# A hybrid decoder layer in float32 on one core: two-operand work moved from GpSimd to VectorE, scan outputs issued later, and four PSUM banks for the gated state-space projection

## The chip, the cores and the metric

The kernel runs on one core of a Trainium2 chip. A core has five engines, each with its own queue of instructions that it works off in order: TensorE (PE, matmuls into PSUM banks), VectorE (DVE), ScalarE (ACT), GpSimd (POOL) and SyncE (SP, which issues transfers). They meet only through semaphores, so an instruction that waits holds up all that stands behind it on its engine. The metric is the time on the device in microseconds, the median of several runs.

## What is computed

A layer with a residual stream of 1024 positions by 1024 channels, all in float32:

```python
mod = silu(c) @ W_ada + b_ada          # shift, scale, gate for two sub-layers
u = rmsnorm(h) * g_mix * (1 + scale1) + shift1
q, k, v, u_ssm, g_att, g_ssm = split(u @ w_in)
y_att = dilated_window_attention(q, k, v) @ w_proj_att     # three patterns, 8 heads
y_ssm = s5(u_ssm) @ w_proj_ssm         # complex diagonal scan, gelu, GLU
merged = sigmoid(g_att) * y_att + sigmoid(g_ssm) * y_ssm
h = h + gate1 * (merged @ w_out)
u = rmsnorm(h) * g_ffn * (1 + scale2) + shift2
a, val = split(u @ w_up)               # 2 x 2048
h = h + gate2 * ((silu(causal_conv3(a)) * val) @ w_down)
out = rmsnorm(h) * g_final
```

## The kernel before

**Float32 products.** [...] So each operand is split into a high part, which ACT makes by a copy with rounding, and a low part, the difference, made by a subtraction with two operands. A product is then three matmuls into one bank (`mm3`, L185): high by high, high by low, low by high (L187 to L189). Every weight goes through this: class `Weights` loads item after item (`_load_to`), splits it two items ahead of its use (`_parts`: ACT at L123, the low part at L124), and chooses the engine for the low part at L111: VectorE for some of the out projection's items, GpSimd for all others.

**Order.** Nothing is scheduled by a tool; the order on each engine is the order in which the program issues. A `Builder` keeps a clock in estimated microseconds (`unit`, L152). The main line of the program adds to it with every group of matmuls, and generators in the background (`spawn`, with a delay) put in their instructions when the clock passes their next due time.

**Stages**, by the time in the trace:

- 0 to 75 us, first products: a loop over 8 channel chunks k (L380). `prep_a(k)` makes the scale of the chunk: `row_dot`, a dot product of a row of `W_ada` with silu(c) on DVE (`ada_dot`, L1413), the bias added (L328), the column `gs` (L346); then ACT scales x by it into the high part of `xg` (L318) and squares x (L355), and GpSimd adds the squares up (L357). `split_w` makes the weights' parts, the low one on GpSimd (L309). `prep_b(k)` makes the low part of `xg` on DVE (L361). PE then does seven groups, 21 matmuls, for the chunk. Eight more dots for the shift come in late (`DOTS`; one of them, `POOL_DOTS`, is multiplied on GpSimd). A matmul with ones (L368) adds up the squares over the partitions, `newton` makes the root, and the bias products (L443) follow.
- 75 to 131: the normalised input u, and its value, query and key products. 134 to 356: attention.
- 356 to 485: gates and projections of the attention branch, in the order g0 g1 g2 p0 p1 p2 g3 p3 and so on to g7 p7. A projection takes its bank (`ps_s`, two of them) and DVE multiplies it into `Tm` (L639). In the background runs the S5 branch: its scan is small DVE instructions (L1736 to L1740) for two halves of the channel groups, one after the other; `outputs(q)` turns the scan's states into outputs on PE (L1749, L1750, the latter reads the scan's result L), and then follow transfers and the gelu.
- 485 to 610: gates of the state-space branch, the GLU, and the merge: `proj_ssm` (L699) takes a bank, multiplies it by the gate (L709), adds `Tm` (L710), and splits the result into high (L711, ACT) and low (L713 on GpSimd, L717 on DVE for the last two tiles). Dots for the second modulation (`adaB`) run on DVE in the background.
- 610 to 700: out projection in two halves; `residual` (L835) adds it to the stream and sums squares (`acc`, L847, on GpSimd there). 700 to 748: first feed-forward blocks and `norm2` for the second half, with low parts (`op_lo`, L825) partly on GpSimd.
- 748 to the end: the feed-forward part by Strassen's scheme, bound by PE, and the final norm.

PSUM has eight banks, two for each of the tags mm, s, t and o (L174).

Of the kernel before, what the change touches and what calls it, by code (L numbers as in the profile page):

```python
# [39 lines left out]
LAG2 = 2  # L40
LOP = (4, 5, 6, 7)
U2A, U2B = 7.5, 3.0
ADA1 = 8.0
FIN, LATE_ACC = 5.0, 3
PREP = 4
# [26 lines left out]
class Weights:  # L72
# [139 lines left out]
def body(tc, I, O, dbg=None):  # L212
    b = Builder(tc, I, O)
    nc = tc.nc
    with ExitStack() as ctx:
# [88 lines left out]
        def split_w(i):  # L304
            raw = raws.pop(i)
            w = b.whl.tile([P, 2, 1024], R32, name="whl", tag="whl") if i in (0, 1, 5) else b.A([P, 2, 1024], R32, "whA")
            for cs in halves if i == 0 else [slice(0, 1024)]:
                nc.scalar.activation(w[:, 0, cs], raw[:, cs], AF.Copy)
                nc.gpsimd.tensor_sub(w[:, 1, cs], raw[:, cs], w[:, 0, cs].bitcast(F32))  # L309
# [10 lines left out]
        def row_dot(j):  # L320
            row = rows.pop(j)
            if j in POOL_DOTS:
                nc.gpsimd.tensor_mul(row, row, csil)
                nc.scalar.activation(row, row, AF.Copy, accum_out=mod[:, j:j + 1])
            else:
                ada_dot(nc, mod, j, row, csil)
            if j >= KT:
                nc.vector.tensor_add(mod[:, j:j + 1], mod[:, j:j + 1], cols[:, j:j + 1])  # L328

# [12 lines left out]
        w0, xg = [], {}  # L342

        def prep_a(k):
            row_dot(KT + k)
            nc.vector.tensor_scalar(gs1[:, k:k + 1], mod[:, KT + k:KT + k + 1], 1.0, cols[:, C_GMIX + k:C_GMIX + k + 1],  # L346
                                    op0=OP.add, op1=OP.mult)
            if k == 0:
                xg_hi(0, halves[:1])
            if k % 2 == 0:  # L350
                w0.append(split_w(k // 2))
            if k:
                xg_hi(k, [slice(0, S)])
            sq = sqp[:, 1 if k else 0]
            nc.scalar.activation(sq, xs[k], AF.Square)  # L355
            if k > 0:
                nc.gpsimd.tensor_add(sqp[:, 0], sqp[:, 0], sq)  # L357

# [13 lines left out]
        late = {}  # L372
        for fn, at in ((row_dot, DOTS), (stats, STATS)):
            for a, kn in enumerate(at):
                late.setdefault(kn, []).insert(0, (fn, a))
# [4 lines left out]
        for k in range(KT):  # L380
# [55 lines left out]
        load_w(6)  # L436
        list(newton[0])

# [261 lines left out]
        def proj_ssm(m, wp, c0):  # L700
# [3 lines left out]
            for hf in range(2):  # L704
                hs = slice(hf * HF, (hf + 1) * HF)
                ps = b.ps("s")
                b.run(b.group(ps, wp, 2, Z, hf, c0))
# [128 lines left out]
        def residual(src, x, m, gate, hs, first, last):  # L836
# [7 lines left out]
            if last:  # L844
                ends.setdefault(hs.start, []).append(sq)
            else:
                (nc.vector if gate == 40 and m % ND >= LATE_ACC else nc.gpsimd).tensor_add(acc[:, hs], sq, acc[:, hs])  # L847

        def norm2(n, hf, tiles, low):

# [8 lines left out]
            if n >= LAG2:  # L859
                op_lo(*tiles[n - LAG2], nc.gpsimd if n - LAG2 in low else nc.vector)  # L860

        def gen_u2a():
# [7 lines left out]
            for n in range(KT + LAG2):  # L870
                norm2(n, 0, tiles, ())
                yield 3.0

        def gen_u2b():
# [17 lines left out]
            for k in range(4):  # L892
# [727 lines left out]
class S5:  # L1620
# [5 lines left out]
    def chain(self, coeff):  # L1626
# [275 lines left out]
```

## Time and profile before

| | |
|---|---|
| Three runs | 1199.57, 1201.26, 1202.49 us; median 1201.26 |
| The profiled execution | 1198.02 us; its span in the trace 1196.2 us |
| Mean clock granted to PE | 0.978 |
| DMA | 155.00 MB, mean 130 GB/s |
| POOL in slices 1 to 10 (tenths busy, 40 slices of 29.9 us) | 5553245545 |

A row of the timeline gives the start, the duration, the engine, the line of the kernel, the operation, the tiles (out<-in) and shapes; in brackets stands how long the engine had been idle before it and what ended that (`<-` engine, tile, line). A row of the list of waits gives the total, the number and the longest. A row of the windows gives the stretch, its length, the busy time of PE, of weight loads (PEld), DVE, ACT and POOL with the number of instructions, then the granted clock, the DMA share and GB/s.

### The profile page before, as it was taken

To read this page: it belongs to the slowest core of one execution; us is meant where nothing else is said; L and a number is where in the kernel's file an instruction comes from. 1 tells how busy PE (TensorE), PEld (TensorE's weight loads), DVE (VectorE), ACT (ScalarE), POOL (GpSimd) and SP (SyncE) were. 2 spreads that over 40 slices of the span, in tenths; PEclk is the share of its full clock that TensorE was granted. 3 is DMA by queue.
4 is the path that set the end of the run, shared out by engine and by line. 5 is a ranking of instruction groups with operands and counts; after the bars stand their busy time and mean duration, and the time that the engine had idled before them with its cause. 6 is when DMAs were issued, how large, how long until landed. Compare 5 with 4: busy or idle time off the path is not lost.

```text
span 1196.2 us, 14783 instructions
## 1 busy us (share of the span) xinstructions
PE 1123.7 (94%) x5276; PEld 920.5 (77%) x5276; DVE 890.0 (74%) x1606; ACT 573.9 (48%) x1041; POOL 323.4 (27%) x259
## 2 busy tenths in 40 slices
PE   8779999999999977999999999899999999999995
PEld 6547788888878866877778887688888888887784
DVE  6898677877549597246876758978886777979767
ACT  4334677777852312332233554644543446635653
POOL 5553245545422211224633653000000000000115
PEclk9889999999999988999999999899999999999998
DMA  9410211111123212125458360254533327769433
GB/s 376 172 36 18 80 53 36 52 38 54 36 63 86 49 58 72 47 102 162 143 185 309 102 229 36 73 174 148 186 125 123 103 84 258 277 230 375 168 124 140
DMA packets 56184, 155.00 MB, mean 130 GB/s; under 512 B 7312, under 2 KB 13584, under 8 KB 54320
## 3 DMA queue, kind: packets, MB, share of 16 engines
q1 hardware_dynamic: 46368, 140.37, 33.1%
q10 hardware_dynamic: 9744, 13.70, 3.6%
q8 instruction: 41, 0.67, 0.2%
q14 instruction: 31, 0.25, 0.1%
HBM read 122.00 MB, written 31.46 MB: 128 GB/s over the span
## 4 chain that ended last, share of the span: by engine, by line
PE 60%; DVE 23%; ACT 8%; issue 3%; DMA 3%; POOL 1%; SPq 0%; DVEq 0%; ACTq 0%; POOLq 0%
PE ps_s L1259 13%; PE ps_mm L1259 9%; PE ps_t L1259 8%; PE ps_mm L187 6%; PE ps_mm L189 6%; PE ps_mm L188 6%; DVE ada L1413 3%; PE ps_s L187 2%; PE ps_s L188 2%; PE ps_s L189 2%; DVE tt L1738 2%; DMA xk<-in_xT 1%; DVE op L825 1%; PE ps_t L1552 1%; ACT S L1528 1%
## 5 line engine op out<-in xcount | busy, mean ns | idle before, releaser
L1259 PE MATMUL ps_s<-op,half 128*128 128x512 f32 x792 | 189.5, 390 | 2.9 <-ACT ps_s L1273 1.9
L1259 PEld LDWEIGHTS ps_s<-op,half 128*128 128x128 f32 x792 | 148.4, 188 | 35.3 <-ACT ps_s L1273 3.2
L124 POOL TENSOR_TENSOR whl<-wraw,whl 128x256 fp32r<-128x256 f32 (+2 forms) x68 | 102.3, 1505 | 197.8 <-ACT whl L123 191.3
L847 POOL TENSOR_TENSOR acc<-tp,acc 128x512 f32<-128x512 f32 x22 | 31.7, 1443 | 455.6 <-ACT tp L843 455.5
L187 PE MATMUL ps_mm<-u,whl 128*128 128x512 f32 x360 | 144.5, 401 | 0.0
L189 PE MATMUL ps_mm<-u,whl 128*128 128x512 f32 x360 | 141.1, 392 | 0.0
L188 PE MATMUL ps_mm<-u,whl 128*128 128x512 f32 x360 | 141.0, 392 | 0.0
L1259 PE MATMUL ps_mm<-op,half 128*128 128x512 f32 x528 | 127.9, 395 | 2.9 <-DVE f L964 2.9
L1259 PEld LDWEIGHTS ps_mm<-op,half 128*128 128x128 f32 x528 | 100.6, 191 | 24.5 <-ACT half L1064 3.3
L1259 PE MATMUL ps_t<-op,half 128*128 128x512 f32 x432 | 103.9, 389 | 0.7 <-ACT tp L1267 0.7
L1259 PEld LDWEIGHTS ps_t<-op,half 128*128 128x128 f32 x432 | 81.0, 188 | 17.9 <-ACT tp L1267 1.1
L189 PEld LDWEIGHTS ps_mm<-u,whl 128*128 128x128 f32 x360 | 67.9, 188 | 14.9
L187 PEld LDWEIGHTS ps_mm<-u,whl 128*128 128x128 f32 x360 | 68.1, 189 | 12.0 <-issue 1.0
L188 PEld LDWEIGHTS ps_mm<-u,whl 128*128 128x128 f32 x360 | 68.1, 189 | 10.5
L1557 DVE TENSOR_TENSOR PT<-ps_t,PT 128x512 fp32r<-128x512 f32 (+1 forms) x80 | 50.6, 633 | 28.5 <-ACT PT L1555 27.8
L1065 DVE TENSOR_TENSOR half<-scr,half 128x512 fp32r<-128x512 f32 x80 | 54.5, 684 | 16.3 <-ACT half L1064 16.1
L1532 POOL TENSOR_SCALAR S<-S,mcol 128x128 f32<-128x128 f32 (+3 forms) x64 | 48.8, 765 | 50.7 <-DVE mcol L1531 28.7
L123 ACT ACTIVATE whl<-wraw 128x256 fp32r<-128x256 f32 (+2 forms) x73 | 49.7, 681 | 23.0 <-PE ps_s L189 19.0
L1528 ACT ACTIVATE S<-S,mcol 128x128 f32<-128x128 f32 (+3 forms) x64 | 49.3, 771 | 14.7 <-DVE mcol L1526 13.1
L1413 DVE CUSTOM_DVE_ANT_0 ada<-ada,cpage 128x1024 f32<-128x1024 f32 x23 | 51.0, 2238 | 5.5 <-DMA ada<-in_wada 5.5
L1064 ACT ACTIVATE half<-scr 128x512 fp32r<-128x512 f32 x80 | 49.0, 625 | 8.6 <-DVE scr L1046 5.5
L1065 DVE TENSOR_TENSOR half<-wraw,half 128x512 fp32r<-128x512 f32 x66 | 45.0, 685 | 8.8 <-ACT half L1064 8.8
(490 smaller groups left out, 2555.3 us busy)
## 6 DMA issues: line engine op xcount, KB each, us to landing
wraw<-in_wup SPq DMA_DIRECT2D x32, 512.0 KB, 3.6
fq<-f SPq DMA_DIRECT2D x16, 1024.0 KB, 5.6
ft<-fq SPq DMA_DIRECT2D x14, 1024.0 KB, 7.5
ada<-in_wada SPq DMA_DIRECT2D x24, 512.0 KB, 8.5
wraw<-in_wdn SPq DMA_DIRECT2D x20, 512.0 KB, 5.7
adaB<-in_wada ACTq DMA_DIRECT2D x16, 512.0 KB, 4.0
wraw<-in_wout SPq DMA_DIRECT2D x16, 512.0 KB, 3.6
hd<-h SPq DMA_DIRECT2D x12, 512.0 KB, 7.5
```

The lines of the kernel that those rows point to most:

```text
L123: nc.scalar.activation(w[:, 0, cs], raw[:, cs], AF.Copy)
L124: lo.tensor_sub(w[:, 1, cs], raw[:, cs], w[:, 0, cs].bitcast(F32))
L187: nc.tensor.matmul(ps, wh, xh, start=first, stop=False)
L188: nc.tensor.matmul(ps, wh, xl, start=False, stop=False)
L189: nc.tensor.matmul(ps, wl, xh, start=False, stop=last)
L1064: nc.scalar.activation(w[:, 0], src, AF.Copy)
L1065: lows.append(lambda: nc.vector.tensor_sub(w[:, 1], src, w[:, 0].bitcast(F32)))
L1259: mm = lambda wp, xp, i: nc.tensor.matmul(ps, w[:, wp, ws], xp[:, cs], start=first and k + i == 0, stop=k == KT // 2 - 1 and i == 2, skip_ ...
L1413: nc.vector.tensor_tensor_reduce(out=a, in0=a, in1=csil, op0=OP.mult, op1=OP.add, scale=1.0, scalar=0.0, accum_out=mod[:, j:j + 1])
L1528: nc.scalar.activation(tl, tl, AF.Exp, bias=mc[:, 0:1], scale=-1.0, accum_out=mc[:, 2:3])
L1532: nc.gpsimd.tensor_scalar(tl, tl, mc[:, 3:4], 0.0, op0=OP.mult, op1=OP.add)
L1557: 0, lambda: nc.vector.tensor_sub(pt[:, 1, :w], tps[:, :w], pt[:, 0, :w].bitcast(F32)))
```

## The change

Six parts; line numbers are those of the kernel before unless they stand in a fence of the order after.

a. **First products.** The low parts of weights (L309) are made on DVE. For the chunk pairs after the first, `split_hi` issues ACT's half ahead of the dot and hands the DVE half back to be issued after `gs`. The square additions (L357) go to DVE, one chunk later (`lag1`). The bias and the one of the scale are added once for all chunks (`base`), so L328 goes. The dot on GpSimd goes to DVE. The first `newton` is issued within the last chunk.

b. **Weights.** From item `i_mrg + 4` on (the gates g3 to g7 of the state-space branch, its projections, the out projection and the first four up items) the low part L124 is made on DVE.

c. **Merge.** `proj_ssm` takes its two halves' banks from two tags, s and t, so four banks in turn; all low parts of `merged` go to DVE, each issued after the next half's multiplication and addition.

d. **Residual.** All square additions L847 go to DVE.

e. **Norm 2.** The low parts that were on GpSimd (four of the second half, four of T2) go to DVE, those of T2 one step later.

f. **Scan outputs.** `outputs(0)` is spawned 12 units after its scan instead of 2, `outputs(1)` 24 after its own, where it was run in line after 2.

```diff
-S5_LAG, S5_Y = 2.0, 2.0
+S5_LAG, S5_Y = 2.0, (12.0, 24.0)
...
-            lo = nc.vector if self.small + 1 < self.ns < self.small + KT + 1 else nc.gpsimd
+            lo = nc.vector if self.ns >= self.vec else nc.gpsimd
...
+        W.wide, W.small, W.vec = i_up, i_out, i_mrg + 4
...
-                nc.gpsimd.tensor_sub(w[:, 1, cs], raw[:, cs], w[:, 0, cs].bitcast(F32))
+                nc.vector.tensor_sub(w[:, 1, cs], raw[:, cs], w[:, 0, cs].bitcast(F32))
...
+        def split_hi(i):
+            raw = raws.pop(i)
+            w = b.whl.tile([P, 2, 1024], R32, name="whl", tag="whl") if i == 1 else b.A([P, 2, 1024], R32, "whA")
+            nc.scalar.activation(w[:, 0], raw, AF.Copy)
+            return w, lambda: nc.vector.tensor_sub(w[:, 1], raw, w[:, 0].bitcast(F32))
...
+        base = pg1.tile([P, KT], F32, name="base")
+        nc.vector.tensor_scalar(base, cols[:, KT:2 * KT], 1.0, None, op0=OP.add)
+        def square(k):
+            sq = sqp[:, 1 if k else 0]
+            nc.scalar.activation(sq, xs[k], AF.Square)
+            if k:
+                lag1.append(lambda: nc.vector.tensor_add(sqp[:, 0], sqp[:, 0], sq))
...
         def prep_a(k):
+            low = None
+            if k and k % 2 == 0:
+                w, low = split_hi(k // 2)
+                w0.append(w)
             row_dot(KT + k)
...
-            if k > 0:
-                nc.gpsimd.tensor_add(sqp[:, 0], sqp[:, 0], sq)
+            if low:
+                low()
+            for fn in lag1:
+                fn()
+            lag1.clear()
+            square(k)
...
-                ps = b.ps("s")
+                ps = b.ps("t" if hf else "s")
...
-                if m < 6:
-                    nc.gpsimd.tensor_sub(mt[:, 1, hs], t, mt[:, 0, hs].bitcast(F32))
-                else:
-                    for fn in lows:
-                        fn()
-                    lows[:] = [lambda mt=mt, t=t, hs=hs: nc.vector.tensor_sub(mt[:, 1, hs], t, mt[:, 0, hs].bitcast(F32))]
+                for fn in lows:
+                    fn()
+                lows[:] = [lambda mt=mt, t=t, hs=hs: nc.vector.tensor_sub(mt[:, 1, hs], t, mt[:, 0, hs].bitcast(F32))]
...
-                (nc.vector if gate == 40 and m % ND >= LATE_ACC else nc.gpsimd).tensor_add(acc[:, hs], sq, acc[:, hs])
+                nc.vector.tensor_add(acc[:, hs], sq, acc[:, hs])
...
-                op_lo(*tiles[n - LAG2], nc.gpsimd if n - LAG2 in low else nc.vector)
+                op_lo(*tiles[n - LAG2], nc.vector)
...
-            if q == 0:
-                b.spawn(outputs(0), S5_Y)
-        yield S5_Y
-        yield from outputs(1)
+            b.spawn(outputs(q), S5_Y[q])
```

How the order on the engines moves is shown at three places. First VectorE in the first products, one chunk of the loop before and two after; before, a chunk is the dot (an ISA instruction and the read of its sum), the bias, `gs` and the low part of `xg`:

```order
L1413 ISA ada,mod<-ada,cpage 128x1024
L1413 ISA mod 128x1
L328 TENSOR_TENSOR mod<-mod,cols 128x1
L346 TENSOR_SCALAR gs_115<-mod,cols 128x1
L361 SCALAR_TENSOR_TENSOR xg<-xk,gs_115,xg 128x1024
```

and after, two chunks, one with a weight to split and one without:

```order
L1427 ISA ada,mod<-ada,cpage 128x1024
L1427 ISA mod 128x1
L360 TENSOR_SCALAR gs_115<-mod,base,cols 128x1
L317 TENSOR_TENSOR whA<-wvx,whA 128x1024
L352 TENSOR_TENSOR sq<-sq 128x1024
L376 SCALAR_TENSOR_TENSOR xg<-xk,gs_115,xg 128x1024
L1427 ISA ada,mod<-ada,cpage 128x1024
L1427 ISA mod 128x1
L360 TENSOR_SCALAR gs_115<-mod,base,cols 128x1
L352 TENSOR_TENSOR sq<-sq 128x1024
L376 SCALAR_TENSOR_TENSOR xg<-xk,gs_115,xg 128x1024
```

The bias row is gone; ahead of each low part of `xg` now stands the square addition (`sq`), and in every second chunk the low part of a weight (`whA`) as well.

Second TensorE at the outputs of the second scan (`ps_t<-L,Vt` reads the scan's result); before, the second group of four stands within the sixth attention projection (`ps_s<-Oat`), and the gate products of g7 (`ps_mm<-u`) follow it:

```order
L187 MATMUL ps_s<-Oat,whl 128x512
L188 MATMUL ps_s<-Oat,whl 128x512
L189 MATMUL ps_s<-Oat,whl 128x512
L1749 MATMUL ps_t<-U_3619,TP 128x128
L1750 MATMUL ps_t<-L,Vt 128x127
L1749 MATMUL ps_t<-U_3619,TP 128x128
L1750 MATMUL ps_t<-L,Vt 128x127
```

after, the outputs stand behind the gate products of the first state-space gate:

```order
L186 MATMUL ps_mm<-u,whl 128x512
L187 MATMUL ps_mm<-u,whl 128x512
L188 MATMUL ps_mm<-u,whl 128x512
L1763 MATMUL ps_t<-U_3612,TP 128x128
L1764 MATMUL ps_t<-L,Vt 128x127
L1763 MATMUL ps_t<-U_3612,TP 128x128
L1764 MATMUL ps_t<-L,Vt 128x127
```

Between the two places lie the rest of the sixth projection, g7, the whole seventh projection and half of that gate, all of which PE now does ahead of the outputs.

Third VectorE in the merge, from one pair of banks to the next; before, a half is a multiplication out of the bank and the addition of `Tm`, with dots (`adaB`) between:

```order
L709 TENSOR_TENSOR sg<-ps_s,sg 128x512
L710 TENSOR_TENSOR sg<-sg,Tm 128x512
L1413 ISA adaB,mod<-adaB,cs 128x1024
L1413 ISA mod 128x1
L709 TENSOR_TENSOR sg<-ps_s,sg 128x512
L710 TENSOR_TENSOR sg<-sg,Tm 128x512
```

after:

```order
L724 TENSOR_TENSOR sg<-ps_t,sg 128x512
L725 TENSOR_TENSOR sg<-sg,Tm 128x512
L729 TENSOR_TENSOR merged<-sg,merged 128x512
L724 TENSOR_TENSOR sg<-ps_s,sg 128x512
L725 TENSOR_TENSOR sg<-sg,Tm 128x512
L729 TENSOR_TENSOR merged<-sg,merged 128x512
L1427 ISA adaB,mod<-adaB,cs 128x1024
```

The banks alternate between s and t, and behind each pair of operations stands the low part of the half before (`merged`).

More of the change, by code (lines that the diff above doesn't have):

```diff
@@ L40 @@
 LAG2 = 2
-LOP = (4, 5, 6, 7)
 U2A, U2B = 7.5, 3.0
 ADA1 = 8.0
-FIN, LATE_ACC = 5.0, 3
+FIN = 5.0
 PREP = 4
@@ L321, in row_dot @@
             row = rows.pop(j)
-            if j in POOL_DOTS:
-                nc.gpsimd.tensor_mul(row, row, csil)
-                nc.scalar.activation(row, row, AF.Copy, accum_out=mod[:, j:j + 1])
-            else:
-                ada_dot(nc, mod, j, row, csil)
-            if j >= KT:
-                nc.vector.tensor_add(mod[:, j:j + 1], mod[:, j:j + 1], cols[:, j:j + 1])
+            ada_dot(nc, mod, j, row, csil)
         def load_x(k):
@@ L342, in body @@
         w0, xg = [], {}
+        base = pg1.tile([P, KT], F32, name="base")
+        nc.vector.tensor_scalar(base, cols[:, KT:2 * KT], 1.0, None, op0=OP.add)
+        lag1 = []
+        def square(k):
[3 more added lines that the diff above has]
+                lag1.append(lambda: nc.vector.tensor_add(sqp[:, 0], sqp[:, 0], sq))
         def prep_a(k):
+            low = None
+            if k and k % 2 == 0:
+                w, low = split_hi(k // 2)
+                w0.append(w)
             row_dot(KT + k)
-            nc.vector.tensor_scalar(gs1[:, k:k + 1], mod[:, KT + k:KT + k + 1], 1.0, cols[:, C_GMIX + k:C_GMIX + k + 1],
-                                    op0=OP.add, op1=OP.mult)
+            nc.vector.tensor_scalar(gs1[:, k:k + 1], mod[:, KT + k:KT + k + 1], base[:, k:k + 1],
+                                    cols[:, C_GMIX + k:C_GMIX + k + 1], op0=OP.add, op1=OP.mult)
             if k == 0:
                 xg_hi(0, halves[:1])
-            if k % 2 == 0:
-                w0.append(split_w(k // 2))
-            if k:
+                w0.append(split_w(0))
+            else:
                 xg_hi(k, [slice(0, S)])
-            sq = sqp[:, 1 if k else 0]
-            nc.scalar.activation(sq, xs[k], AF.Square)
-            if k > 0:
-                nc.gpsimd.tensor_add(sqp[:, 0], sqp[:, 0], sq)
+            if low:
[4 more added lines that the diff above has]
+            square(k)
         def prep_b(k):
@@ L372, in body @@
         late = {}
-        for fn, at in ((row_dot, DOTS), (stats, STATS)):
+        for fn, at in ((row_dot, DOTS), (stats, STATS), (lambda h2: list(newton[h2]), NEWTON)):
             for a, kn in enumerate(at):
@@ L392, in body @@
             elif k == 6:
+                lag1.pop()()
                 load_w(4)
@@ L436, in body @@
         load_w(6)
-        list(newton[0])
         bps = b.ps("o")
@@ L846, in residual, with norm2 @@
             else:
-                (nc.vector if gate == 40 and m % ND >= LATE_ACC else nc.gpsimd).tensor_add(acc[:, hs], sq, acc[:, hs])
-        def norm2(n, hf, tiles, low):
+                nc.vector.tensor_add(acc[:, hs], sq, acc[:, hs])
+        def norm2(n, hf, tiles):
             hs = halves[hf]
@@ L870, in gen_u2a @@
             for n in range(KT + LAG2):
-                norm2(n, 0, tiles, ())
+                norm2(n, 0, tiles)
                 yield 3.0
@@ L886, in gen_u2b @@
             for n in range(KT + LAG2):
-                norm2(n, 1, xs2, LOP)
+                norm2(n, 1, xs2)
                 if n < KT:
@@ L897, in gen_u2b @@
                 op_hi("T2", k, x22[k])
-                op_lo("T2", k, x22[k], nc.gpsimd)
+                if k:
+                    op_lo("T2", k - 1, x22[k - 1], nc.vector)
                 yield T2P
+            op_lo("T2", 3, x22[3], nc.vector)
             diff.update(T1=x11, T3=x12, T4=x21)
```

4 lines of the change are left out of this document (1 added, 3 removed).

## Prediction

> **What bounds the kernel now.** First the page: the busy time of each engine and the chain of waits that ended last.
>
> ```profile
> PE 1123.7 (94%) x5276; PEld 920.5 (77%) x5276; DVE 890.0 (74%) x1606; ACT 573.9 (48%) x1041; POOL 323.4 (27%) x259
> ...
> PE 60%; DVE 23%; ACT 8%; issue 3%; DMA 3%; POOL 1%; SPq 0%; DVEq 0%; ACTq 0%; POOLq 0%
> ```
>
> TensorE (PE) is busy for 94% of 1196.2 us, so about 72 us of it are waits, and a gain can come only from those waits and from slow restarts behind them. VectorE (DVE) carries 23% of the chain and GpSimd (POOL) 1%: POOL is hardly ever waited for directly. The windows by stage (PE, weight load, DVE, ACT, POOL busy; then the clock granted) say where the idle time lies.
>
> ```profile
> 40.00:75.00 35.00, 25.21 (x86) 18.67 (x85) 32.15 (x34) 11.95 (x13) 20.26 (x7) 0.84 0.11 39
> 75.00:131.00 56.00, 53.03 (x215) 38.98 (x215) 47.73 (x77) 27.44 (x61) 19.48 (x12) 0.94 0.10 33
> ...
> 485.00:610.00 125.00, 117.77 (x507) 95.36 (x506) 72.05 (x78) 38.40 (x56) 50.90 (x25) 0.99 0.38 126
> 610.00:700.00 90.00, 89.51 (x390) 72.83 (x389) 64.30 (x69) 40.22 (x55) 42.53 (x22) 1.00 0.50 183
> ...
> 800.00:1100.00 300.00, 300.00 (x1325) 248.37 (x1324) 241.31 (x397) 143.37 (x267) 0.00 (x0) 1.00 0.53 187
> ```
>
> From 800 to 1100 PE never stops: 1325 matmuls in 300 us, 0.2264 us each. That is the price of a matmul below, and nothing in that stage can gain. From 40 to 75, 86 matmuls took 35 us at a clock of 0.84; at 0.2264 they are 19.5. From 485 to 610 PE lost 7.2 us. (A row's first number is its window, then its length.) Next I read the timelines of those stages, and the list of waits for each.
>
> **The first products (parts a and d of the change there).** The largest wait of ACT up to 80 us, then rows of DVE, of POOL and of PE.
>
> ```profile
> ACT xg L318 <- DVE gs L346: 29.2, 7, 5.3
> ```
>
> ```profile
> 6.47 1.22 DVE L1413 CUSTOM_DVE_ANT_0 ada<-ada,cpage 128x1024 f32<-128x1024 f32 x1 [5.47 <-DMA ada<-in_wada]
> ...
> 31.11 3.42 DVE L1413 CUSTOM_DVE_ANT_0 ada<-ada,cpage 128x1024 f32<-128x1024 f32 x1
> ...
> 34.57 2.21 DVE L328 TENSOR_TENSOR mod<-mod,cols 128x1 f32<-128x1 f32 x1
> 36.81 0.21 DVE L346 TENSOR_SCALAR gs<-mod,cols 128x1 f32<-128x1 f32 x1
> 38.24 1.28 DVE L361 SCALAR_TENSOR_TENSOR xg<-xk,gs,xg 128x1024 fp32r<-128x1024 f32 x1 [1.22 <-ACT xg L318]
> ...
> 45.71 3.42 DVE L1413 CUSTOM_DVE_ANT_0 ada<-ada,cpage 128x1024 f32<-128x1024 f32 x1
> ...
> 620.69 1.23 DVE L124 TENSOR_TENSOR whA<-wraw,whA 128x1024 fp32r<-128x1024 f32 x1 [1.65 <-ACT whA L123]
> ```
>
> ```profile
> 30.89 2.55 POOL L357 TENSOR_TENSOR sq<-sq 128x1024 f32<-128x1024 f32 x1 [3.74 <-ACT sq L355]
> 33.40 3.36 POOL L309 TENSOR_TENSOR whA<-wvx,whA 128x1024 fp32r<-128x1024 f32 x1
> ```
>
> ```profile
> 9.48 0.49 PE L187 MATMUL ps_s<-xg,whl 128*128 128x512 f32 x1
> ...
> 38.26 0.49 PE L187 MATMUL ps_s<-xg,whA 128*128 128x512 f32 x1 [2.19 <-ACT xg L318]
> ...
> 40.49 0.63 PE L188 MATMUL ps_s<-xg,whA 128*128 128x512 f32 x1
> ...
> 63.64 1.62 PE L368 MATMUL ps_o<-sq,nones 128*128 128x512 f32 x2 [3.19 <-POOL sq L357]
> ...
> 74.92 0.59 PE L443 MATMUL ps_o<-whl,shl 128*2 128x512 f32 x1 [3.72 <-DVE tp L1385]
> ```
>
> The same dot product of a row with the condition (L1413) takes 1.22 us at 6.47, when POOL does nothing, and 3.42 at 31.11, when POOL adds squares from 30.89 on; the 128x1 addition at 34.57 takes 2.21 while POOL splits a weight from 33.40 to 36.76. So DVE is held up for as long as a POOL operation with two inputs runs, and the chain dot, addition, gs, ACT's xg, DVE's xg feeds PE. Two chunks take 45.71 - 31.11 = 14.60 us, 7.30 each, and PE's 21 matmuls only 4.75.
>
> After the change POOL does nothing here. DVE then has per chunk: dot 1.22, gs 0.21, xg 1.28, the square addition and, in every second chunk, the low part of a weight. Both of these are 128x1024 subtractions or additions that the trace has on DVE at 1.23 (620.69). That is 3.94 or 5.17, 4.56 in the mean, under PE's 4.75: PE sets the step, with 4% to spare. The path: PE's first matmul at 9.48; the two low halves of the first weight now stand ahead of xg on DVE, 1.2 late; 8 chunks of 4.75 are 38.0; 1.6 for the ones-matmul as in its row at 63.64; 2.0 for DVE's start in series at the third chunk and 1.3 for the last square addition, which DVE does after two shift dots and xg. That is 53.6. Then four shift dots stand behind the Newton steps on DVE, which leave about 2.3 past the last matmul: the bias products begin at 55.9 where the row has 74.92. **Gain 19.0.** Upper end 22 (the 3.3 of waits don't come); lower end 9.4, if the step only falls halfway, from 7.30 to 6.1: 8 x 1.2. I take 19 because the mean of the durations in the rows lies under PE's. Three low parts of the value weights (1.23 each) also go to DVE between 75 and 131; the cover is PE's 215 matmuls there, 48.7 of 56 us, and without it they would cost 3.7.
>
> One rule can be weighed here. The Trainium skill, page "TensorE: Matmul & The Clock Gate", section "HAM oscillation", asks for no gap of PE over about 3.4 us. The trace differs: after a wait of 2.19 at 38.26 the matmul at 40.49 lasts 0.63, not 0.39. By the page the 2.0 I leave at the third chunk costs nothing more; by that row it costs about 2 more, and the lower end covers it.
>
> **Scan outputs (part f).** PE, DVE and POOL around the second scan.
>
> ```profile
> 434.62 0.79 PE L1750 MATMUL ps_t<-L,Vt 128*128 128x127 f32 x2 [8.22 <-DVE L L1740]
> ...
> 463.41 0.79 PE L1750 MATMUL ps_t<-L,Vt 128*128 128x127 f32 x2 [8.26 <-DVE L L1740]
> ```
>
> ```profile
> 452.03 2.39 DVE L1739 TENSOR_TENSOR L<-L,tt 128x56 f32<-128x56 f32 x1
> 454.46 0.26 DVE L1740 TENSOR_TENSOR L<-L,tt 128x56 f32<-128x56 f32 x1
> ...
> 463.27 0.68 DVE L639 TENSOR_TENSOR Tm<-ps_s,Tm 128x512 f32<-128x512 f32 x1
> ```
>
> ```profile
> 451.92 2.40 POOL L124 TENSOR_TENSOR whl<-wraw,whl 128x1024 fp32r<-128x1024 f32 x1 [24.96 <-ACT whl L123]
> ```
>
> PE stood twice, 8.22 and 8.26 us, at the output matmuls, because they had been issued ahead of other work while DVE still scanned. Issued later (12 and 24 units of the builder's clock), both waits go, and so does one of the two slow restarts, an estimate of 2 us (some eight matmuls at 0.63 for 0.39, as at 40.49): 18.5. What is late next: the scan itself doesn't move, and DVE takes the additions into Tm (L639) for the sixth attention projection only after it (463.27). In the new order PE reaches the seventh projection, which needs that bank, after 48 more gate matmuls: 463.41 - 8.26 - 8.22 - 2.0 + 48 x 0.2264 = 455.8. DVE is done at 463.27 + 0.68, plus the locks that the next two weight splits, still on POOL, lay into the scan when PE runs ahead: one lengthened L1739, at 452.03, to 2.39, where its twin L1740 took 0.26. One such and one of half the width, 2.1 + 1.1, make it 467.1. The new wait is 11.3. **Gain 18.5 - 11.3 = 7.2**; upper end 10.5 without the locks; lower end 4, if the later outputs make the gelu and with it the glu late by 3.
>
> **Glu, merge (parts b and c).** The wait list of 485 to 611, DVE, POOL, and PE at the glu.
>
> ```profile
> PE ps_s L187 <- DVE sg L709: 5.4, 5, 1.3
> ```
>
> ```profile
> 520.64 2.74 DVE L1821 TENSOR_TENSOR tp<-tp,z 128x512 f32<-128x512 f32 x1 [26.01 <-ACT tp L1819]
> ...
> 579.23 1.21 DVE L1413 CUSTOM_DVE_ANT_0 adaB<-adaB,cs 128x1024 f32<-128x1024 f32 x1
> ...
> 587.71 2.50 DVE L710 TENSOR_TENSOR sg<-sg,Tm 128x512 f32<-128x512 f32 x1
> ...
> 590.84 0.69 DVE L710 TENSOR_TENSOR sg<-sg,Tm 128x512 f32<-128x512 f32 x1
> ```
>
> ```profile
> 587.27 2.39 POOL L124 TENSOR_TENSOR whl<-wraw,whl 128x1024 fp32r<-128x1024 f32 x1 [3.46 <-ACT whl L123]
> ```
>
> ```profile
> 524.67 0.59 PE L187 MATMUL ps_mm<-zh,whl 128*128 128x512 f32 x1 [2.23 <-ACT tp L1819]
> ```
>
> The glu's product at 520.64 takes 2.74, where 128x512 in two operands takes 0.69 (590.84), and PE waits 2.23 for what follows it. With the split on DVE the lock goes: **gain 2.0**, between 0 (the later gelu eats it) and 3. In the merge PE waits 5.4 in five pieces for the bank that L709 must empty, and L709 stands behind L710, 2.50 under a POOL split and 0.69 without. With four banks in turn and no lock the waits go if DVE keeps up. A step of one gate tile and two projections is 72 matmuls, 16.3 us; on DVE it is 4 x (0.69 + 0.69 + 0.69) for L709, L710 and the low part, 1.23 and about 0.7 for the two weights, 4 dots of 1.22 (579.23): 15.1. **Gain 5.0**, between 0 (DVE late) and 5.5.
>
> **Norm 2 and the tail (parts d and e).**
>
> ```profile
> PE ps_s L188 <- POOL op L825: 1.7, 3, 0.7
> ```
>
> ```profile
> 744.92 1.67 DVE L894 TENSOR_TENSOR x<-x 128x512 f32<-128x512 f32 x1
> ```
>
> ```profile
> 750.94 5.53 PE L1259 MATMUL ps_mm<-op,half 128*128 128x512 f32 x12 [2.87 <-DVE f L964]
> ...
> 1178.29 1.70 PE L1259 MATMUL ps_mm<-op,sw 128*128 128x256 f32 x12 [1.63 <-DVE hh L838]
> ...
> 1181.97 0.70 PE L1372 MATMUL ps_o<-acc,nones 128*128 128x256 f32 x2 [0.54 <-POOL acc L847]
> ```
>
> PE waits three times, 1.7 together, for POOL's low parts; an addition of 0.69 (as at 590.84) takes 1.67 at 744.92, locked; the wait of 2.87 at 750.94 is followed by 12 matmuls in 5.53, twice their price. Eight low parts move to DVE, 8 x 0.69 = 5.5, and take the place of the locks. The most is 1.7 + 2.87 + 2.8 = 7.4; I take less than half, **3.0** (0 to 6), since DVE's queue before 750 doesn't become shorter. In the tail the square additions leave POOL: of 1.63 and 0.54 **2.0** go (1 to 2.5); the last POOL work, on the output, stays.
>
> The splits and additions of the out projection (610 to 700) I cost at nothing: PE is busy 89.51 of the 90 us there by the windows above, and DVE, at 64.30, has a quarter free. Without that cover it is a rival below.
>
> **Sum.** 19.0 + 7.2 + 2.0 + 5.0 + 3.0 + 2.0 = 38.2. The profiled execution took 1198.02 us (span 1196.2 and 1.8 around it) and would take 1159.8. The median of the three runs, 1201.26, lies 3.2 above it; 1201.26 - 38.2 = **1163**. All lower ends give 9.4 + 4 + 0 + 0 + 0 + 1 = 14.4, all upper ends 49.5.
>
> **Rivals.**
>
> *DVE keeps up everywhere.* The locks laid into the second scan don't come and the first products have no waits: 22 + 10.5 and the rest as above, 44.5, 1157; with all upper ends 1152. For it: POOL loses over half of its work, so fewer splits fall on DVE. Against: the scan itself ends where it ended. Chance 0.13.
>
> *DVE becomes the bound.* It is busy 74% and gets 72 us of moved work (32 operations of 1.23 and 48 of 0.69), while its locked time goes. In the first products it has 4% to spare, in the merge 7%; one late row each turns both into DVE's step. Then the first products gain 9.4, merge and norm 2 nothing: 9.4 + 7.2 + 2 + 2 = 20.6, 1181. Against: the 3.42 and 2.21 of today already count as DVE's. Chance 0.14. The Trainium skill, page "Perfetto Trace Analysis", section "Optimizing Scalar/DVE Operations", says that work may well go to GpSimd when DVE is saturated, which speaks against this change, and adds that the shared port can spoil it. The trace bears out the second half (3.42 against 1.22).
>
> *Slower: heads of the queue.* A low part on DVE waits for ACT's high part, and everything behind it on DVE waits too: the row at 620.69 stood 1.65 us. 22 weight splits and 4 of the value weights are moved. If each holds DVE for 1.65 and PE stands for a bank that DVE should empty, 26 x 1.65 = 43, more than the gain: 1206. It decides from a slack on DVE under 1.65 per split; the merge has 1.2 by the sum above, the out projection and the value products more. Chance 0.05.
>
> *The change doesn't do what it says.* If the dots are slow because DMA fills their rows and not because of POOL, the first products stay: 19.2 for the rest, 1182. Against: 34.57 reads 128x1 and is just as late. Chance 0.03.
>
> **How the numbers follow.** The forecast, between 1157 and 1172, has 0.65. Range: from 1153, most of the first rival, to 1179, short of the DVE-bound case; left out are that case's far half, the slow one and the last, and a little of the first, about 2 in 10 at most. A change of 0.2% (2.4 us, what a measurement of this kernel can tell from none) is outside all cases but the last rivals' edges: faster 0.94, same 0.01, slower 0.05.
>
> **What would show it.** Right: dots of 1.22 throughout the first products, a step of 4.8, bias products near 56; no wait at the output matmuls; a wait near 11 at the seventh projection behind Tm; no waits on sg in the merge. Wrong: a step over 5.2, DVE waiting for ACT's high parts with PE idle behind it, or glu waits of more than 3.

## The result, and the profile after

The changed kernel takes 1166.63 us (median of four runs, 1164.78 to 1168.23), the kernel before 1200.41 (four runs, 1195.63 to 1202.49). The ratio is 0.9724, with a 95% interval of 0.9691 to 0.9757: 33.8 us or 2.8% less. The forecast was 1163, in a range of 1153 to 1179.

The profiled execution took 1168.23 us, the longest of the four, with a span of 1166.4; the one before took 1198.02 with a span of 1196.2. The two traces therefore show 29.8 of the 33.8, which the interval (29.2 to 37.1 us) allows.

The page of the changed kernel, the busy times and the chain of waits:

```profile
PE 1113.7 (95%) x5276; PEld 916.2 (79%) x5276; DVE 883.3 (76%) x1681; ACT 574.0 (49%) x1039; POOL 158.5 (14%) x178
...
PE 66%; DVE 18%; ACT 8%; DMA 5%; issue 3%; SPq 0%; DVEq 0%; ACTq 0%
```

POOL has lost half of its work (323.4 to 158.5 us) and DVE is as busy as before (890.0 to 883.3): by the prediction's count, an estimate, 72 us of work went over, so about as much of DVE's earlier time went away. DVE's share of the chain fell from 23% to 18%.

Where the time came from is read off the same places of PE's timeline in both traces. Each stage ends with the first (or last) matmul named:

| stage, up to PE's | before | after | gain in it | forecast |
|---|---|---|---|---|
| bias products | 74.92 | 58.25 | 16.7 | 19.0 |
| first attention projection | 347.17 | 329.66 | 0.8 | 0 |
| glu | 518.20 | 492.65 | 8.0 | 7.2 |
| first state-space projection | 549.60 | 522.32 | 1.7 | 2.0 |
| first matmul of the out projection | 610.77 | 576.72 | 6.8 | 5.0 |
| its last | 699.86 | 669.91 | -4.1 | 0 |
| first Strassen product | 750.94 | 717.60 | 3.4 | 3.0 |
| end of the span | 1196.2 | 1166.4 | -3.5 | 2.0 |
| sum | | | 29.8 | 38.2 |

Two stages became slower. First the rows that answer to those of the prediction; VectorE in the first products of the changed kernel (new line numbers: dot L1427, gs L360, square addition L352, xg L376):

```profile
26.53 1.22 DVE L1427 CUSTOM_DVE_ANT_0 ada<-ada,cpage 128x1024 f32<-128x1024 f32 x1
...
29.11 1.22 DVE L352 TENSOR_TENSOR sq<-sq 128x1024 f32<-128x1024 f32 x1
30.25 1.28 DVE L376 SCALAR_TENSOR_TENSOR xg<-xk,gs,xg 128x1024 fp32r<-128x1024 f32 x1
31.44 1.22 DVE L1427 CUSTOM_DVE_ANT_0 ada<-ada,cpage 128x1024 f32<-128x1024 f32 x1
...
35.40 1.22 DVE L1427 CUSTOM_DVE_ANT_0 ada<-ada,cpage 128x1024 f32<-128x1024 f32 x1
```

```profile
10.65 0.50 PE L186 MATMUL ps_s<-xg,whl 128*128 128x512 f32 x1 [1.48 <-ACT whl L307]
...
13.18 0.79 PE L187 MATMUL ps_s<-xg,whl 128*128 128x512 f32 x1 [2.03 <-DVE xg L376]
...
58.25 0.40 PE L458 MATMUL ps_o<-whl,shl 128*2 128x512 f32 x1 [3.29 <-DVE shl L450]
```

All dots take 1.22. Two chunks take 35.40 - 26.53 = 8.87 us, where they took 14.60: 4.44 each, so DVE is ahead of PE's 4.75. PE waits 2.03 at the first chunk, for the low halves of the weight, and 3.29 at the bias products, for the last four shift dots.

TensorE and VectorE at the end of the second scan:

```profile
449.42 0.77 PE L186 MATMUL ps_s<-Oat,whl 128*128 128x512 f32 x1 [11.32 <-DVE Tm L654]
```

```profile
440.16 2.48 DVE L1750 TENSOR_TENSOR tt<-L,AA 128x248 f32<-128x248 f32 x1
...
447.99 0.68 DVE L1754 TENSOR_TENSOR L<-L,tt 128x504 f32<-128x504 f32 x1
448.59 1.28 DVE L654 TENSOR_TENSOR Tm<-ps_s,Tm 128x512 f32<-128x512 f32 x2
```

```profile
439.84 2.43 POOL L123 TENSOR_TENSOR whl<-wraw,whl 128x1024 fp32r<-128x1024 f32 x1 [8.14 <-ACT whl L122]
```

The two waits at the outputs (8.22 and 8.26) are gone, and the new one stands where the prediction put it, at the seventh projection behind the additions into Tm, 11.32 us long; the row at 440.16, 2.48 for a product that takes about 0.6, is one of the locks laid into the scan: DVE is held up while POOL splits a weight, from 439.84 to 442.27. The glu's product on DVE, and PE behind it:

```profile
495.67 1.08 DVE L1832 TENSOR_TENSOR tp<-tp,z 128x512 f32<-128x512 f32 x1
```

```profile
498.04 0.50 PE L186 MATMUL ps_mm<-zh,whl 128*128 128x512 f32 x1 [1.14 <-ACT tp L1830]
...
500.43 0.50 PE L186 MATMUL ps_mm<-u,whl 128*128 128x512 f32 x1 [0.74 <-ACT tp L1830]
```

The product takes 1.08 in place of 2.74, and PE waits 1.14 and 0.74 where it waited 2.23 once. The start of the out projection, before and after:

```profile
610.77 0.47 PE L187 MATMUL ps_s<-merged,whA 128*128 128x512 f32 x1 [0.37 <-DVE sg L709]
```

```profile
582.72 0.51 PE L186 MATMUL ps_s<-merged,whA 128*128 128x512 f32 x1 [1.07 <-ACT merged L726]
...
584.59 0.50 PE L187 MATMUL ps_s<-merged,whA 128*128 128x512 f32 x1 [1.36 <-DVE merged L729]
...
586.00 0.63 PE L186 MATMUL ps_mm<-merged,whl 128*128 128x512 f32 x1
```

```profile
579.45 1.23 DVE L123 TENSOR_TENSOR whl<-wraw,whl 128x1024 fp32r<-128x1024 f32 x1 [1.05 <-ACT whl L122]
580.59 0.68 DVE L724 TENSOR_TENSOR sg<-ps_s,sg 128x512 f32<-128x512 f32 x1
```

DVE stood 1.05 for ScalarE's half of the next weight (L123), and the evacuations of the last merged tile (L724) came after it. PE waited 1.07 and 1.36, and soon after seven matmuls ran at 0.63. In the tail:

```profile
1147.80 1.89 PE L1273 MATMUL ps_mm<-op,sw 128*128 128x256 f32 x11 [2.82 <-DVE hh L850]
```

```profile
1137.53 0.74 DVE L850 SCALAR_TENSOR_TENSOR hh<-ps_mm,mod,hh 128x512 f32<-128x512 f32 x1
1138.97 1.30 DVE L859 TENSOR_TENSOR acc<-tp,acc 128x512 f32<-128x512 f32 x1 [0.70 <-ACT tp L855]
...
1143.92 0.69 DVE L859 TENSOR_TENSOR acc<-tp,acc 128x512 f32<-128x512 f32 x1 [0.70 <-ACT tp L855]
```

These square additions (L859) on DVE wait 0.70 each for ScalarE, and the evacuations behind them wait too; PE's wait at the same place was 1.63 and is 2.82.

### The profile page after: what moved, and what is told of

It reads as the page before. It is cut to its first block, busy times and chain, and to the rows that moved or that the text cites. A ratio compares the mean times of both kernels' runs of the same rounds, so it can differ in the third digit from the quotient of the medians.

```text
span 1166.4 us, 14714 instructions
## 1 busy us (share of the span) xinstructions
PE 1113.7 (95%) x5276; PEld 916.2 (79%) x5276; DVE 883.3 (76%) x1681; ACT 574.0 (49%) x1039; POOL 158.5 (14%) x178
## 4 chain that ended last, share of the span: by engine, by line
PE 66%; DVE 18%; ACT 8%; DMA 5%; issue 3%; SPq 0%; DVEq 0%; ACTq 0%
PE ps_s L1273 12%; PE ps_mm L1273 9%; PE ps_mm L186 7%; PE ps_mm L188 7%; PE ps_mm L187 7%; PE ps_t L1273 7%; PE ps_s L187 3%; PE ps_s L186 3%; PE ps_s L188 3%; PE ps_t L1566 2%; PE ps_s L1530 1%; PE ps_o L1583 1%; ACT op L833 1%; PE ps_s L1531 1%; DMA hd<-h 1%
## 5 line engine op out<-in xcount | busy, mean ns | idle before, releaser
L1273 PEld LDWEIGHTS ps_s<-op,half 128*128 128x128 f32 x792 | 148.1, 188 | 37.1 <-ACT ps_s L1287 2.9
L1375 POOL TENSOR_TENSOR hh<-hh,acc 128x512 f32<-128x512 f32 x3 | 4.2, 1439 | 650.2 <-DVE acc L1400 650.2
L123 POOL TENSOR_TENSOR whl<-wraw,whl 128x256 fp32r<-128x256 f32 (+2 forms) x52 | 63.8, 1227 | 140.4 <-ACT whl L122 134.0
L1569 ACT ACTIVATE PT<-ps_t 128x512 fp32r<-128x512 f32 (+1 forms) x80 | 43.7, 550 | 10.3 <-PE ps_t L1566 9.2
```

Of the source, the lines that this page charges most:

```text
L123: lo.tensor_sub(w[:, 1, cs], raw[:, cs], w[:, 0, cs].bitcast(F32))
L1273: mm = lambda wp, xp, i: nc.tensor.matmul(ps, w[:, wp, ws], xp[:, cs], start=first and k + i == 0, stop=k == KT // 2 - 1 and i == 2, skip_ ...
L1569: nc.scalar.activation(pt[:, 0, :w], tps[:, :w], AF.Copy)
```

## The experiments

Times are medians; the kernel before took 1197.5 to 1199.0 beside them, a little less than beside the changed kernel alone. Unless said otherwise an experiment is an edit of the changed kernel, and 1166.6 is what it stands against. Since the kernel before moved by up to 2.9 us between these series, a difference of about 2 us between medians says little by itself, and the stages in the traces must bear it out.

### First products: the engine and the order

```diff
-                nc.vector.tensor_sub(w[:, 1, cs], raw[:, cs], w[:, 0, cs].bitcast(F32))
+                nc.gpsimd.tensor_sub(w[:, 1, cs], raw[:, cs], w[:, 0, cs].bitcast(F32))
...
-            return w, lambda: nc.vector.tensor_sub(w[:, 1], raw, w[:, 0].bitcast(F32))
+            return w, lambda: nc.gpsimd.tensor_sub(w[:, 1], raw, w[:, 0].bitcast(F32))
...
-                lag1.append(lambda: nc.vector.tensor_add(sqp[:, 0], sqp[:, 0], sq))
+                lag1.append(lambda: nc.gpsimd.tensor_add(sqp[:, 0], sqp[:, 0], sq))
```

> The changed kernel, with the low parts of the first and the value weights and the square additions of the first products on GpSimd again; the new order (additions one chunk late, no bias row, all dots on VectorE) stays. Theory (the lock: a two-operand GpSimd operation holds VectorE up): the dots go back to about 3.4 us in the first products, the bias products begin 12 to 17 us later than the 58.25 of the changed kernel, and the time rises from 1166.6 to 1179 to 1184. Rival (it was the order, with the bias row and the late additions, that shortened the chain): the bias products begin within 4 us of 58.25 and the time stays under 1171.

It took 1176.61 us (ratio to the kernel before 0.9814, 0.9799 to 0.9829). The bias products began at 66.70, 8.45 later: neither theory. VectorE and GpSimd in it:

```profile
21.13 3.41 DVE L1427 CUSTOM_DVE_ANT_0 ada<-ada,cpage 128x1024 f32<-128x1024 f32 x1
...
28.03 1.21 DVE L1427 CUSTOM_DVE_ANT_0 ada<-ada,cpage 128x1024 f32<-128x1024 f32 x1
...
32.55 3.41 DVE L1427 CUSTOM_DVE_ANT_0 ada<-ada,cpage 128x1024 f32<-128x1024 f32 x1
```

```profile
29.15 2.40 POOL L317 TENSOR_TENSOR whA<-wvx,whA 128x1024 fp32r<-128x1024 f32 x1 [2.12 <-ACT whA L316]
31.50 3.38 POOL L352 TENSOR_TENSOR sq<-sq 128x1024 f32<-128x1024 f32 x1
```

The lock is there, 3.41 while POOL works from 29.15 to 34.88, but in every second chunk only. Two chunks take 32.55 - 21.13 = 11.42, so 5.71 each, in place of 7.30. With the additions one chunk late and the bias row gone, half of the gain stays without a change of engine. So the opposite was tried, on the kernel before: the engine alone.

```diff
-                nc.gpsimd.tensor_sub(w[:, 1, cs], raw[:, cs], w[:, 0, cs].bitcast(F32))
+                nc.vector.tensor_sub(w[:, 1, cs], raw[:, cs], w[:, 0, cs].bitcast(F32))
...
-                nc.gpsimd.tensor_add(sqp[:, 0], sqp[:, 0], sq)
+                nc.vector.tensor_add(sqp[:, 0], sqp[:, 0], sq)
...
-POOL_DOTS = (4,)
+POOL_DOTS = ()
```

> The kernel before, with the weights' low parts, the square additions and the one dot of the first products on VectorE, and nothing else changed: the additions stand right behind ScalarE's square, the bias row stays. Theory (the engine alone is worth little, because the addition now waits for the square on VectorE's queue, some 2.3 us per chunk, ahead of the next chunk's low part): the step per chunk is 6.5 to 7.3 us, the bias products begin at 70 to 75, time 1195 to 1200. Rival (engine and order each bring their half): the bias products begin at 66 to 68, time 1189 to 1192.

It took 1191.12 us (0.9945, 0.9925 to 0.9965), 6.4 less than the kernel before, and its bias products began at 68.27, against 74.92. That is the rival, if 0.3 past its place for the bias products: each part brings about half, 6.7 and 8.2, and together they bring 16.7. (The dot that leaves GpSimd counts in both.) Its row shows what the order is for:

```profile
25.68 1.22 DVE L1413 CUSTOM_DVE_ANT_0 ada<-ada,cpage 128x1024 f32<-128x1024 f32 x1
...
29.52 1.23 DVE L357 TENSOR_TENSOR sq<-sq 128x1024 f32<-128x1024 f32 x1 [2.17 <-ACT sq L355]
30.66 1.28 DVE L361 SCALAR_TENSOR_TENSOR xg<-xk,gs,xg 128x1024 fp32r<-128x1024 f32 x1
31.85 1.22 DVE L1413 CUSTOM_DVE_ANT_0 ada<-ada,cpage 128x1024 f32<-128x1024 f32 x1
```

The dots are free of locks, but the addition waits 2.17 us for the square on DVE's queue. The chunk takes 31.85 - 25.68 = 6.17; one chunk later, in the changed kernel, there is no wait, and 4.44.

### Scan outputs and the new wait

```diff
-S5_LAG, S5_Y = 2.0, (12.0, 24.0)
+S5_LAG, S5_Y = 2.0, (2.0, 2.0)
```

> The changed kernel with both scan outputs spawned 2 units after their scans. Theory (the two old waits were traded for one at the seventh projection): two waits of about 8 us at the output matmuls come back, the wait of 11.3 at the seventh projection goes, the glu starts 5 to 8 us later, time 1172 to 1175. Rival (the issue time of the outputs is worth nothing, since PE waits for the second scan in any case): the glu starts within 2 us of 492.65, time 1165 to 1169.

```profile
415.86 0.80 PE L1764 MATMUL ps_t<-L,Vt 128*128 128x127 f32 x2 [8.22 <-DVE L L1754]
```

```profile
444.53 0.79 PE L1764 MATMUL ps_t<-L,Vt 128*128 128x127 f32 x2 [8.29 <-DVE L L1754]
```

It took 1175.21 us; the two waits are back, the one at the seventh projection is gone, the glu starts 6.6 later, as the theory had it. So the change traded two waits for one. Next, whether that one can go. First by pacing the scan on the builder's clock as it runs:

```diff
-S5_LAG, S5_Y = 2.0, (12.0, 24.0)
+S5_LAG, S5_Y = 2.0, (3.0, 3.0)
...
-                yield 2.5 if cnt > 32 else 1.2 if cnt > 16 else 0.6
+                yield 0.75 + 0.0425 * cnt
```

> The changed kernel with the scan's steps spaced on the builder's clock by what they take on VectorE in the trace (0.75 us and 0.0425 per column in place of 2.5, 1.2 and 0.6), and the outputs 3 units after each scan. Theory (the wait of 11.3 at the seventh projection exists only because the scan is paced too fast, so that all of it stands ahead of the additions into Tm): the additions now stand inside the scan, the wait falls under 2 us, the outputs wait under 2, the glu starts 7 to 10 us earlier than 492.65, time 1157 to 1160. Rival (the scan itself ends too late for the gelu, so the wait moves to the glu): the glu starts within 3 us of 492.65, time 1164 to 1167.

```profile
462.82 0.79 PE L1764 MATMUL ps_t<-L,Vt 128*128 128x127 f32 x2 [9.89 <-DVE L L1754]
```

```profile
444.01 1.21 DVE L1806 TENSOR_TENSOR gw<-yb 128x1024 f32<-128x1024 f32 x1
...
453.67 2.61 DVE L1750 TENSOR_TENSOR tt<-L,AA 128x248 f32<-128x248 f32 x1
...
462.08 0.68 DVE L1754 TENSOR_TENSOR L<-L,tt 128x504 f32<-128x504 f32 x1
```

It took 1165.81 us, the same as the changed kernel within the run's noise. The wait at the projection is gone, but not into the glu, as the rival had it: it moved to the outputs, 9.89. The scan's last row L1754 starts at 462.08 and not at 447.99. Most of these 14.1 us are the gelu of the first half, which now stands on DVE ahead of the scan's last two steps, from 444.01 to 453.67; in the changed kernel it came behind the scan. So the gain of the theory didn't come; what the slower pace would bring with the outputs left late wasn't run. Then by another bank:

```diff
-                        ps = b.ps("s")
+                        ps = b.ps("o" if m == 7 else "s")
                         yield from b.group(ps, w, 4, Oa, hf)
```

> The changed kernel with the two halves of the seventh attention projection in the banks of the tag o, which nothing else uses at that time. Theory (the wait of 11.3 is a wait for a bank alone; the scan on VectorE ends at 448.7 in any case and PE would come to its outputs at about 449): the wait goes, the outputs wait under 2 us, the glu starts 10 to 12 us earlier than 492.65, time 1154 to 1157. Rival (the gelu of the second half is too late, so PE waits at the glu instead): a wait of 6 or more at the glu, time 1160 to 1165.

```profile
459.70 0.50 PE L186 MATMUL ps_mm<-u,whl 128*128 128x512 f32 x1 [1.62 <-ACT sg L707]
...
461.86 0.50 PE L188 MATMUL ps_mm<-u,whl 128*128 128x512 f32 x1 [1.42 <-POOL whl L123]
```

It took 1157.58 us, 9.1 less. PE ends the attention projections 13.0 earlier and the outputs don't wait. 3.6 of it are lost again right after, in two waits of 1.62 and 1.42, for the evacuation of a gate (ACT) and for the low part of a weight (POOL). The glu is not late: its wait is 1.14, as before. The wait of 11.3 was a wait for a bank and nothing else. The glu starts 9.4 earlier, and the time lies 0.6 over the theory's range, both a little short of it.

### The merge: banks, engine and weights

```diff
-                ps = b.ps("t" if hf else "s")
+                ps = b.ps("s")
```

> The changed kernel with the state-space projection's halves both from the tag s, two banks in turn as before. Theory (in the merge the lock was the cause and the banks are only cover): waits of PE for sg of 1 to 2 us in all, time 1167 to 1169. Rival (the banks are the cause): the five waits of about 1.3 come back, time 1170 to 1173.

```profile
528.70 0.50 PE L186 MATMUL ps_s<-zsh,whl 128*128 128x512 f32 x1 [2.02 <-DVE sg L724]
...
529.90 0.63 PE L187 MATMUL ps_s<-zsl,whl 128*128 128x512 f32 x1
...
548.93 0.50 PE L186 MATMUL ps_s<-zsh,whl 128*128 128x512 f32 x1 [2.02 <-DVE sg L724]
```

```profile
523.00:592.00 69.00, 61.81 (x245) 48.07 (x243) 47.88 (x74) 19.03 (x29) 0.00 (x0) 0.93 0.42 137
```

It took 1181.76 us, 15.1 more, beyond both theories. With all low parts on DVE two banks give waits of 2.02, and behind each of them some eight slowed matmuls, most at 0.63: the clock in the window is 0.93. The same 245 matmuls, in windows of the changed kernel and of the kernel before:

```profile
522.00:577.00 55.00, 55.00 (x245) 45.53 (x244) 46.34 (x72) 18.07 (x27) 0.00 (x0) 1.00 0.52 166
```

```profile
549.00:611.00 62.00, 56.64 (x245) 45.23 (x244) 52.02 (x55) 19.48 (x29) 37.87 (x19) 1.00 0.47 152
```

55.0 us, 69.0 with two banks, 62.0 before. Moving the low parts without the banks makes the merge 7 slower than before; with them it is 7 faster.

```diff
+                if m < 6:
+                    nc.gpsimd.tensor_sub(mt[:, 1, hs], t, mt[:, 0, hs].bitcast(F32))
+                    continue
                 for fn in lows:
                     fn()
```

> The changed kernel with the low parts of the first six merged tiles on GpSimd again, four banks kept. Theory (the lock makes VectorE late in the merge): rows of L725 over 1 us, from the first merge product to the out projection 2 to 5 us longer, time 1168 to 1171. Rival (four banks cover the locks): the stretch stays within 1 us, time 1165 to 1168.

It took 1172.02 us, 5.4 more, 1.0 past the theory's range. Its mark is there, but weak: of the 16 rows of L725 six are over 1 us, 1.05 to 1.07. From the first state-space projection to the out projection it is 1.3 longer, less than the theory's 2 to 5, and the start of the out projection waits 1.82 and 1.37 instead of 1.07 and 1.36. That makes the out projection 1.9 longer; another 1.7 lies behind the first Strassen product, which the edit doesn't touch. So the edit itself is shown to cost about 3.

```diff
-            lo = nc.vector if self.ns >= self.vec else nc.gpsimd
+            lo = nc.vector if self.small + 1 < self.ns < self.small + KT + 1 else nc.gpsimd
```

> The changed kernel with the low parts of the weights of the merge, the out projection's first two and second half, and the first up items on GpSimd again. Theory (they lock VectorE, and that costs more than the waits for ScalarE that they bring to VectorE's queue): rows of 2 us and more on VectorE in the merge and before the first up blocks, time 1169 to 1174. Rival (heads of the queue: on VectorE they hold up the evacuations behind them, as at the start of the out projection, 3 to 4 us): time 1162 to 1166.

It took 1168.77 us (1168.37 to 1174.02), 2.1 more and between the two theories. Rows of VectorE in it:

```profile
496.37 2.74 DVE L1832 TENSOR_TENSOR tp<-tp,z 128x512 f32<-128x512 f32 x1 [9.40 <-ACT tp L1830]
...
562.30 2.57 DVE L725 TENSOR_TENSOR sg<-sg,Tm 128x512 f32<-128x512 f32 x1
```

The locks are back in the glu (2.74) and the merge (2.57), and four banks cover the merge: it takes as long as in the changed kernel (54.4). The glu costs 3.8 and the first up blocks 1.9. (The profiled run was its slowest, 1174.02.) Part b is worth about 2 us by the medians, no more than the kernel before moved between series; that it works in these two stages is what the trace shows.

### The two losses

```diff
-                nc.vector.tensor_add(acc[:, hs], sq, acc[:, hs])
+                (nc.vector if gate != 40 or m % ND >= 3 else nc.gpsimd).tensor_add(acc[:, hs], sq, acc[:, hs])
```

> The changed kernel with the square additions of the last residual (the feed-forward one, but not its last tile) on GpSimd again, as before. Theory (each such addition on VectorE waits 0.70 us for ScalarE's square and holds up the evacuations behind it, so the tail became slower and not faster): the wait of 2.82 in the tail falls to about 1.6, the end comes 2 to 4 us earlier, time 1163 to 1165. Rival (the locks return and cost as much): 1166 to 1168.

```profile
1143.91 1.70 PE L1273 MATMUL ps_mm<-op,sw 128*128 128x256 f32 x12 [1.63 <-DVE hh L850]
```

It took 1164.31 us, 2.3 less, as the theory had it. The wait is back at 1.63, and from the first Strassen product to the end it takes 444.7 us, against 448.8 in the changed kernel and 445.3 before. A part of that is the run: the nine traces with these additions on DVE take 446.8 to 450.6 there, the five with them on POOL 444.6 to 446.4, so the engine makes 3.0 in the mean.

```diff
-                    if n == len(merge_order) - 1:
-                        W.prefetch(iw + n + 3)
         b.drain()
         for fn in lows:
             fn()
+        W.prefetch(iw + len(merge_order) + 2)
```

> The changed kernel with the split of the out projection's second weight issued behind the merge's last low part instead of between the last two tiles. Theory (that split, waiting for ScalarE on VectorE's queue, holds up the last two merged halves): the waits of 1.07 and 1.36 at the start of the out projection go with the slow matmuls behind them, from its first to its last matmul 89 to 91 us in place of 93.2, time 1162 to 1165. Rival (the weight comes too late instead): PE waits 1 us or more for the second weight, time 1165 to 1168.

```profile
PE ps_mm L188 <- DVE whl L123: 0.5, 1, 0.5
PE ps_s L187 <- DVE merged L729: 0.5, 1, 0.5
```

It took 1164.45 us, 2.2 less, again with the theory. Of the two waits 0.5 is left, another 0.5 for the weight is new, and the out projection takes 90.7 in place of 93.2. The out projection took 89.1 before, so 1.6 of its loss stays open. Both losses have the same mark: an operation on DVE that waits for ScalarE, with evacuations behind it.

### Together

> The changed kernel with three edits: the seventh attention projection in the banks of the tag o, the last residual's square additions on GpSimd, the out projection's second weight split behind the merge. Theory (the three costs lie in different stages and add up: 9.1, 2.3 and 2 to 4): time 1151 to 1154. Rival (they share a bound, so that one only uncovers the next): 1154 to 1157.

The three edits (banks of the tag o, tail on GpSimd, late split) give 1153.60 us: 13.0 less than the changed kernel, ratio 0.9631 (0.9617 to 0.9646) to the kernel before. Alone they gave 9.1, 2.3 and 2.2, together 13.6: they add up.

```diff
-        W.wide, W.small, W.vec = i_up, i_out, i_mrg + 4
+        W.wide, W.small, W.vec = i_up, i_out, i_mrg + 1
```

> The three edits together and, besides, the low parts of the state-space gates from the second on made on VectorE. Theory (PE's wait of 1.42 for GpSimd's low part behind the scan outputs and the lock on the glu go): 1 to 3 us less than without, 1149 to 1152. Rival (VectorE has the gelu to do there and makes the low part later than GpSimd would): the same or up to 3 more.

```profile
461.48 0.50 PE L188 MATMUL ps_mm<-u,whl 128*128 128x512 f32 x1 [1.58 <-DVE whl L123]
```

It took 1155.91 us, 2.3 more than without: the rival. PE now waits 1.58 for DVE's low part where it waited 1.42 for POOL's. There DVE has the gelu, and the weight is no earlier. In the traces the two are 0.2 apart up to the first Strassen product, so it isn't shown that the edit costs the 2.3.

## Why the prediction came out as it did

The forecast time held: 33.8 us gained against 38.2 by the sum. Most of the causes were those named, but one term had the wrong sign, one that stood at nothing cost 4.1, and others had a part of their cause wrong. By the traces the sum was 8.4 too large (29.8). The medians hide 4.0 of that, because the profiled execution lies 2.4 below the median before and 1.6 above it after. Step by step:

- **First products, 19.0 against 16.7.** That PE sets the step was right (4.44 on DVE, 4.75 on PE). Short by 1.0 at the loop's end (54.57 against 53.6) and by 1.4 at the four shift dots (3.29 of wait); but in the eleven traces with this stage unchanged the bias products begin at 55.7 to 58.3, so the forecast 55.9 lies among them and the profiled run is the latest. The cause given was half of the truth: the prediction laid the whole gain on the lock. The runs give about half to the order, with the bias row gone and the additions a chunk late.
- **Scan outputs, 7.2 against 8.0.** The new wait was forecast at 11.3 and measured at 11.32, at the place and behind the instruction named. Its two ends were right, too, and didn't just fit by luck: PE came 17.7 and DVE's addition ended 17.8 earlier than the 455.8 and 467.1 named, as the whole was 17.5 ahead by then. Undoing this part costs 8.6. What the step didn't see is that a free pair of banks takes the wait away.
- **Glu and merge.** The glu came to 1.7 (forecast 2.0), but less by the wait than forecast: the product takes 1.08 without the lock and not the 0.69 it was compared with, and two waits of 1.88 together stand for the one of 2.23. The rest is the slow restart behind that one, seven matmuls of 0.63 or more from 525.06 on; in the changed kernel none is over 0.50 there. The merge came to 6.8 (5.0), but the step that put the lock and the banks together was wrong in its weights: without the banks the merge loses 7 us, with the banks the locks of weight splits cost it nothing and those of the merged tiles 1.3.
- **The out projection, forecast at nothing, lost 4.1.** The step that failed is "I cost at nothing: PE is busy 89.51 of the 90 us there". That cover is right for the stage, but its start isn't covered: there the last merged tile must come through DVE's queue, and the split placed between the last two tiles waits for ScalarE. This is the rival of the queue's heads, at one place. Issuing that split later brings 2.5 of the 4.1 back; 1.6 stay open. The Trainium skill, page "Perfetto Trace Analysis", section "Optimizing Scalar/DVE Operations", speaks of moving work off a DVE that is saturated. That is not the case here: DVE is no busier than before (883.3 against 890.0 us), and what costs is the order on it.
- **The tail, forecast at +2.0, cost 3.5 with the feed-forward part.** The sign was wrong. The step took POOL's additions for the cause of the wait of 1.63; on DVE they wait 0.70 each, and the wait grew to 2.82. With them on POOL the same wait is 1.63 again. Over all fourteen traces the loss is 3.0 in the mean.
- **Norm 2, 3.0 against 3.4.** The size was right, the cause only in part. PE's three waits for POOL's low parts are gone, as forecast. But with the weights' low parts back on GpSimd the stage loses 1.9 again, so over half of the 3.4 belongs to part b, which the step didn't count there. The norm's own low parts weren't moved back alone.

The rival in which DVE becomes the bound (1181) needed a chunk step of 6.1; it is 4.44. That the change does nothing to the dots falls with rows of 1.22 throughout. DVE's keeping up everywhere fell at the second scan: a locked row stood in it again, and the wait had its forecast length.

## What to carry to other kernels

Moving work off an engine that locks another pays in full only if its input is ready when its turn comes on the new queue: in the first products the engine alone brought 6.7 of 16.7 us with the addition right behind its producer, and in the tail additions placed so lost 3.0. Before a wait is removed by issuing later, ask what stands behind the same queue next, and whether a bank lies idle for it. A stage that is covered by PE on the whole need not be covered at its first matmuls.

## What the runs showed of the hardware

Waits of about 2 us cost more than themselves. In the merge before, five waits of up to 1.3 (5.4 together) left the clock at 1.00; with two banks three waits of 2.02 and two shorter ones (7.2 together) brought it to 0.93, with some eight slowed matmuls, most at 0.63, behind each of the three. At the start of the out projection waits of 1.07 and 1.36 with one matmul between them were followed by seven at 0.63. The Trainium skill, page "TensorE: Matmul & The Clock Gate", section "HAM oscillation", gives about 3.4 us as the longest idle gap to allow; here 2.02 was too long, so the measurement decides. The Trainium skill, page "Perfetto Trace Analysis", section "Matmul Optimizations", says to "Ensure all 8 PSUM banks are being leveraged": the runs agree, with 15.1 us for the merge's second pair and 9.1 for the seventh projection's.
